# Whole weight rows for the first down product, stores on POOL's queue, sums on DVE

## The chip, the cores and the metric

The kernel runs on one core of a Trainium2 chip. The metric is device time in microseconds (us), of which the median of three runs is given. A profile of one further execution shows what each engine did when: TensorE (PE; its weight loads are shown as PEld), VectorE (DVE), ScalarE (ACT), GpSimd (POOL) and SyncE (SP), which in the kernel before issues all transfers. Each engine works through its own instructions in order.

## The reference

One step of a one-layer streaming encoder, for a prompt of 1024 positions and for 8 running streams of 16 positions each ("sample", 128 rows together). All arithmetic is in fp32.

```python
x = x + rmsnorm_pair(attention(h), s5_glu(h)) @ w_out      # h = rmsnorm(x) @ w_in
up = rmsnorm(x) @ w_up                                     # 1024 -> 2 x 2816
c = sum(up_padded[:, j:j+L] * conv_w[j] for j in range(3)) + conv_b
gate, val = split(c, 2)
x = x + (silu(gate) * val) @ w_down                        # 2816 -> 1024
y = rmsnorm(x) * final_g
```

Beside y it returns the new attention cache rows, the new state of the S5 recurrence and the new state of the convolution (the last two rows of `up` of each stream). The change touches the last three lines: how `w_down` is loaded and combined, how the gated values `g = silu(gate) * val` are stored and added, how the convolution's rows are stored, and how the last norms are scheduled.

## The kernel before

**Two stages matter here.** The up stage runs over 22 pairs `j` (one block of 128 gate columns and one of 128 value columns). Each pair is seven products (`product`, `collect`); `prep` splits the weights of the products ahead. In step 2 of the next pair `up_pair_end` does the convolution, the gate and the product g, and stores g to a scratch tensor: `g_d` for the prompt, `gs_d` for the sample. The down stage multiplies g (2816 long, 22 blocks, seen as two halves of `NK` = 11 blocks) with `w_down`.

**Splits.** A matmul of full precision is three matmuls on rounded operands (`mm3`): high times high, high times low, low times high. So each operand is first split in two: ACT writes the rounded high part (`wh`, `gh`), DVE subtracts it to get the low part (`wl`, `gl`). `operand` (lines 1522 to 1532) does this; the DVE half runs through the helper `tt` at line 86.

**The down product by seven.** The prompt's part is a 2 x 2 block product in seven products instead of eight (the Strassen-Winograd form). With the quarters g11 to g22 of g and B11 to B22 of `w_down`, the kernel runs them in this order: B11 with g11, T1 with S1, T2 with S2, B22 with S4, T3 with S3, B21 with g12, T4 with g22. Each is a loop over k of 11 steps with 12 matmuls of 512 columns a step. S1 is the sum of two quarters (`sum_one`, on POOL), and S2, S4 come from it by subtraction on DVE; S3 is the subtraction in the B22 loop at line 1710, `gr<-gr,gr` in the profile. T1 to T4 are sums of weight quarters: during the up stage `wd_load` fetches a block of them, `wd_sums` adds it up on DVE and stores it to the scratch tensor `t_d`, one block for each pair, 22 in all, in one buffer `ws`.

**The first product** (called the first down product below, lines 1643 to 1668) does two things at each step k: `p1_pairs` multiplies B11 with g11 for the prompt, and `p1_sample` multiplies all four quarters with the sample's g, which is too small to be worth the seven-product form. So it reads the whole of `w_down`, in blocks of 128 x 512 (256 KB): `w_op` loads a block into one of `WDB` = 5 buffers `wd` and splits it. The blocks B11 and B12 of a step are the two halves of the same 128 rows of 1024, as are B21 and B22.

**Order.** The program is written in one order, and a planner then orders the instructions of each engine by a simulated time: it may bring an instruction forward past ones written earlier, where its inputs are ready by its own estimate. `with tc.issue_after(x)` forbids it to put the block's instructions ahead of x on that engine. On the chip the order is fixed, and an instruction that waits holds up all behind it on its engine or queue. All transfers before are issued by SP, so a transfer that waits for a buffer holds up the following ones.

**Other pieces.** `conv_out` transposes the rows of the convolution state on TensorE, copies them with DVE into one of two buffers `cvr`, and stores them (seven times). The residual tiles `x3_0` to `x3_8` (128 x 1024) are loaded by `load_x` during T1 and T2, and a finished output is added to them by `drain`. `half_one` and `half_two` do the last norm: squares on ACT, the reciprocal root with a chain of small DVE operations (`rstd`), and the scaling. In the last product T4 the last five steps are held back and run tile by tile (`ops`), so that four row tiles finish one after the other.

```python
nc.sync.dma_start(g_d[j], g[:, 0:SEQ])
wd_sums(j - 1)                       # in pair j, step 1;  wd_load(j) in step 4
raw = dwA.tile([P, 512], F32, name=f"wd{w}", tag=f"wd{w % WDB}")
nc.gpsimd.tensor_tensor(SU[k], GA[1, 0, k], GA[1, 1, k], op=OP.add)
tt(GA[1, 0, k], GA[0, 0, k], GA[1, 0, k], OP.subtract)
half_two((NP2 + p,), HI, LO)
```

Of the kernel before, what the change touches and what calls it, by code (L numbers as in the profile page):

```python
# [18 lines left out]
P = 128  # L19
# [26 lines left out]
def emit(ctx, tc, x_prompt, x_sample, cache_k, cache_v, state_ssm_re, state_ssm_im, state_conv,  # L46
# [10 lines left out]
    def f(ap):  # L57
        return ap.bitcast(F32)
# [1342 lines left out]
    def up_pair_end(j):  # L1401
        cg = upw.tile([P, GLEN], F32, name=f"cg{j}", tag="cg", bufs=1)
        up_conv(j, 0, cg)
        act(cg, cg, AF.Silu)
        g = upw.tile([P, GLEN], F32, name=f"g{j}", tag="gs")
        up_conv(j, 1, g)
        tt(g, g, cg, OP.mult)
        nc.sync.dma_start(g_d[j], g[:, 0:SEQ])
        nc.sync.dma_start(gs_d[:, j], g[:, SEQ:])


    NK = NF // 2
# [40 lines left out]
    for i in range(7):  # L1453
        product(i, 1, pl0)
        collect(i, 1)
        prep(7 + i)
        if i == 3:
            wd_load(0)
    ps1.close()
    pups = ExitStack()  # L1460
    pup = pups.enter_context(pool("pup", 8, space=PSUM))
    for j in range(1, NF):
        load_up(j + 1)
        up_begin(j)
        for i in range(7):
            n = 7 * j + i
            for g in range(2):
                product(n, g)
                collect(n, g)
            prep(n + 7)  # L1470
            if i == 2:
                up_pair_end(j - 1)
            if i == 1:
                with tc.issue_after(LOW[min(n + 7, 7 * NF - 1)].ins):
                    wd_sums(j - 1)
            if i == 4:
                with tc.issue_after(UR[min(j + 1, NF - 1)].ins):
                    wd_load(j)
    wd_sums(NF - 1)
    up_pair_end(NF - 1)  # L1480
    fu.close()
    exs.close()
# [31 lines left out]
                    GS[q, k + i] = t[:, q, i]  # L1514

    def load_x(t):
        X3[t] = gr.tile([P, DM], F32, name=f"x3_{t}")
        nc.sync.dma_start(X3[t], x2_d[t * P:(t + 1) * P])

    CW, CG, SPARE, WD = [0], [0], [], {}  # L1520

    def operand(src, base, count, bufs, spare):
        w = count[0]
        count[0] += 1
        n = src.shape[-1]
        if spare:
            hi, lo = (gr.tile([P, n], F32R, name=f"{base}{x}{w}", tag=SPARE.pop()) for x in "hl")
        else:
            hi, lo = (dwA.tile([P, n], F32R, name=f"{base}{x}{w}", tag=f"{base}{x}{w % bufs}") for x in "hl")
        act(hi, src, AF.Copy)  # L1530
        tt(lo, src, f(hi), OP.subtract)
        return hi, lo

    def w_op(blk, k, spare=False):
        w = CW[0]
        raw = dwA.tile([P, 512], F32, name=f"wd{w}", tag=f"wd{w % WDB}")
        if blk[0] == "T":
            src = t_d[k, :, SUM_AT[blk]]
        else:
            r, e = (int(blk[1]) - 1) * NK + k, int(blk[2]) - 1  # L1540
            src = w_down[0, r * P:(r + 1) * P, e * 512:e * 512 + 512]
        WD[0] = nc.sync.dma_start(raw, src)
        return operand(raw, "w", CW, 4, spare)

    def g_op(src, spare=False):
        return operand(src, "g", CG, 2, spare)
# [4 lines left out]
    def conv_out():  # L1551
        cf = cvt.rearrange("p r a -> p (r a)")
        n = NROW * NF2
        outp = [(conv_prompt[0, 0].rearrange("j (a p) -> (j a) p", p=P), 0, 2 * NF2),
                (conv_sample[0].rearrange("b j (a p) -> (b j a) p", p=P), 2 * NF2, n - 2 * NF2)]
        for dst, c0, m_ in outp:
            for i in range(0, m_, P):
                m = min(P, m_ - i)
                pt = pdn.tile([P, P], F32, name=f"cvo{c0}_{i}", tag=f"b{(i // P) % 2}")
                nc.tensor.transpose(pt[:m], cf[:, c0 + i:c0 + i + m], ident)  # L1560
                r = dw.tile([P, P], F32, name=f"cvr{c0}_{i}", tag="rows", bufs=2)
                V_.tensor_copy(r[:m], pt[:m])
                nc.sync.dma_start(dst[i:i + m], r[:m])

    LO, HI = slice(0, 512), slice(512, DM)
    S3 = dw.tile([P, 2, NT], F32, name="S3")
# [43 lines left out]
    def sum_one(k):  # L1610
        if k < NK:
            SU[k] = gr.tile([P, 512], F32, name=f"su{k}", tag=f"su{k}")
            nc.gpsimd.tensor_tensor(SU[k], GA[1, 0, k], GA[1, 1, k], op=OP.add)


    smb, w11 = {}, {}

    def p1_pairs(k):
        w11[k] = w_op("B11", k)
        g = g_op(GA[0, 0, k])  # L1620
        for p in range(NP2):
            c = slice(p * P, (p + 1) * P)
            last = mm3(bank("a", p, k == 0), g[0][:, c], g[1][:, c], *w11[k], k == 0, k == NK - 1)
        return last

    def p1_sample(k):
# [8 lines left out]
        if k == 0:  # L1635
            for e in range(2):
                smb[e] = pdn.tile([P, 512], F32, name=f"dns{e}", tag=f"b{2 + e}")
        for blk in ("B11", "B12", "B21", "B22"):
            w = w11[k] if blk == "B11" else w_op(blk, k)
            q, e = int(blk[1]) - 1, int(blk[2]) - 1  # L1640
            mm3(smb[e], *sm[q], *w, k == 0 and q == 0, k == NK - 1 and q == 1)

    for k in range(NK):
# [62 lines left out]
    for k in range(NK):  # L1706
        w = w_op("B22", k)
        g = g_op(SU[k])
        pairs("b", k, g, w, False)
        tt(GA[1, 0, k], GA[0, 0, k], GA[1, 0, k], OP.subtract)  # L1710
        SPARE.append(f"su{k}")
    for p in range(NP2):
        drain("a", p, 0, HI)
# [33 lines left out]
    for p in range(NP2):  # L1747
        for k, (g, w) in ops.items():
            pairs("a", k, g, w, False, p)
        drain("a", p, 1, LO)  # L1750
        half_two((NP2 + p,), HI, LO)


_INS = ['x_prompt', 'x_sample', 'cache_k', 'cache_v', 'state_ssm_re', 'state_ssm_im', 'state_conv',
# [27 lines left out]
```

## Time and profile before

| what | us |
|---|---|
| median of 3 runs (lowest to highest) | 1218.39 (1217.08 to 1219.61) |
| the profiled execution's own time | 1217.93 |
| its span, first to last instruction | 1216.2 |
| TensorE busy in the span | 1161.7 |
| DVE busy | 943.3 |
| ACT busy | 658.2 |
| POOL busy | 256.6 |

All times in the text count from the start of the span. The up stage's last matmul is issued at about 949, the first down product runs to about 1020, T1 to about 1055, and the last matmul ends at 1205.7. A row of a view by stretches gives the stretch and its length, then for each engine busy time and number of instructions, then TensorE's granted clock as a share of full speed, the DMA engines' busy share, and GB/s. A row of waits reads: engine and tile, what it waited for, the total in us, how often, the longest. A row of a timeline gives start and duration in us, engine, line, operation, output and inputs, shapes. Names follow the kernel: `dna` and `dnb` are the down product's PSUM banks, `dns` the sample's, `su` the sums, `gr` the loaded quarters of g, `wd` the raw weights, `x` the residual tiles.

### The profile page before, as it was taken

The numbers are of one execution on the slowest core, as the hardware profiler recorded it, in microseconds if no ns is written. First come the engines' busy times: TensorE is split into PE (matmuls) and PEld (weight loads), VectorE is DVE, ScalarE is ACT, GpSimd is POOL, SyncE is SP. The second block draws the span as 40 slices with busy tenths as digits, with TensorE's granted clock in tenths as the row PEclk, the third lists the DMA queues.
The fourth block names the chain that finished last, engine by engine and source line by source line (L and its number), as shares of the span: only waits on it lengthen the run. The fifth ranks groups of instructions, "written<-read, shape, count | busy, mean of one in ns | idle before, by whom it ended". The sixth has DMA issues, their size and how long they took to land. (4 is left out here: it accounts for less than half of the span.)

```text
span 1216.2 us, 20649 instructions
## 1 busy us (share of the span) xinstructions
PE 1161.7 (96%) x7396; PEld 1022.7 (84%) x7396; DVE 943.3 (78%) x2061; ACT 658.2 (54%) x1417; POOL 256.6 (21%) x287
## 2 busy tenths in 40 slices
PE   8899999899989987999999999999999999999996
PEld 6777777677878767999999999999999776788885
DVE  6799768798437977887878878878787768977665
ACT  7246556763385776445455445454454555446553
POOL 0000000000000202644545545546442013000000
PEclk9899999899999989999999999999999999999998
DMA  8523226667723430334334243343333799842333
GB/s 256 111 81 129 91 69 179 201 210 210 216 70 139 140 136 29 115 116 139 104 126 141 90 142 126 110 140 108 127 125 118 247 309 332 302 139 92 96 102 139
DMA packets 165032, 177.89 MB, mean 146 GB/s; under 512 B 30618, under 2 KB 122402, under 8 KB 164898
## 3 DMA queue, kind: packets, MB, share of 16 engines
q1 hardware_dynamic: 164930, 176.58, 45.4%
q8 instruction: 58, 0.95, 0.3%
q14 instruction: 44, 0.36, 0.1%
HBM read 124.36 MB, written 53.23 MB: 146 GB/s over the span
## 5 line engine op out<-in xcount | busy, mean ns | idle before, releaser
L1307 DVE TENSOR_TENSOR op<-ur,op 128x512 fp32r<-128x512 f32 x132 | 121.7, 924 | 79.9 <-ACT op L1306 79.7
L1306 ACT ACTIVATE op<-ur 128x512 fp32r<-128x512 f32 x132 | 83.0, 632 | 92.0 <-POOL ur L1257 42.4
L1257 POOL TENSOR_TENSOR S<-ur 128x512 f32<-128x512 f32 x22 | 42.4, 1926 | 234.6 <-DMA ur<-in_w_up_dram 234.1
L1530 ACT ACTIVATE wh<-wd 128x512 fp32r<-128x512 f32 x110 | 68.4, 628 | 29.3 <-DMA wd<-in_w_down_dram 8.0
L86 DVE TENSOR_TENSOR wl<-wd,wh 128x512 fp32r<-128x512 f32 x110 | 74.2, 684 | 6.4 <-ACT wh L1530 6.3
L62 PE MATMUL dna<-wl,gh 128*128 128x512 f32 x176 | 70.1, 398 | 0.0
L61 PE MATMUL dna<-wh,gh 128*128 128x512 f32 x176 | 64.2, 396 | 3.9 <-ACT wh L1530 3.9
L1395 POOL COPY cvt<-ext 128x2 f32<-128x2 f32 x44 | 30.4, 690 | 158.4 <-DVE ext L86 158.4
L86 DVE TENSOR_TENSOR ws<-ws 128x256 f32<-128x256 f32 x88 | 56.1, 637 | 0.8 <-DVE ext L86 0.4
L63 PE MATMUL dna<-wh,gl 128*128 128x512 f32 x176 | 55.3, 397 | 0.0
L86 DVE TENSOR_TENSOR gl<-gr,gh 128x512 fp32r<-128x512 f32 x44 | 30.6, 695 | 30.8 <-PE dna L63 12.1
L62 PE MATMUL dnb<-wl,gh 128*128 128x512 f32 x132 | 50.4, 393 | 1.7 <-DVE wl L86 1.6
L61 PE MATMUL dnb<-wh,gh 128*128 128x512 f32 x132 | 49.0, 392 | 1.5 <-ACT wh L1530 0.9
L1530 ACT ACTIVATE gh<-gr 128x512 fp32r<-128x512 f32 x44 | 27.6, 630 | 36.4 <-PE dna L62 23.4
L1396 POOL COPY cvt<-ext 128x16 f32<-128x16 f32 x44 | 32.8, 746 | 63.4 <-ACT ext L1366 63.4
L1399 DVE SCALAR_TENSOR_TENSOR cg<-ext,cw,cg 128x1168 f32<-128x1168 f32 x22 | 44.5, 2022 | 0.0
L61 PEld LDWEIGHTS dna<-wh,gh 128*128 128x128 f32 x176 | 32.9, 189 | 11.8 <-ACT wh L1530 5.1
L1530 ACT ACTIVATE gh<-su 128x512 fp32r<-128x512 f32 x33 | 20.8, 632 | 36.7 <-PE dnb L62 19.0
L1257 POOL TENSOR_TENSOR ur<-S,ur 128x512 f32<-128x512 f32 x22 | 37.0, 1681 | 17.2 <-DVE op L1307 17.1
L62 PEld LDWEIGHTS dna<-wl,gh 128*128 128x128 f32 x176 | 34.0, 193 | 7.7 <-DVE wl L86 0.4
L63 PEld LDWEIGHTS dna<-wh,gl 128*128 128x128 f32 x176 | 33.9, 193 | 7.3
L1106 POOL MEMSET L<- 128x8 f32 x4 | 0.2, 112 | 181.1 <-PE pkv L62 181.1
(1278 smaller groups left out, 4366.9 us busy)
## 6 DMA issues: line engine op xcount, KB each, us to landing
ur<-in_w_up_dram SPq DMA_DIRECT2D x44, 512.0 KB, 4.7
wd<-in_w_down_dram SPq DMA_DIRECT2D x66, 256.0 KB, 3.8
ws<-in_w_down_dram SPq DMA_DIRECT2D x44, 256.0 KB, 3.4
g_d<-g SPq DMA_DIRECT2D x22, 512.0 KB, 2.6
t_d<-ws SPq DMA_DIRECT2D x22, 512.0 KB, 3.2
gr<-g_d SPq DMA_DIRECT2D x44, 256.0 KB, 6.1
wd<-t_d SPq DMA_DIRECT2D x44, 256.0 KB, 3.0
wa<-a_d SPq DMA_DIRECT2D x9, 512.0 KB, 3.5
```

Source lines behind the costliest of these rows:

```text
L61: mm(out, lh, rh, start=first, stop=False, skip_group_check=True)
L62: mm(out, lh, rl, start=False, stop=False, skip_group_check=True)
L63: return mm(out, ll, rh, start=False, stop=last, skip_group_check=True)
L86: V_.tensor_tensor(o, a, b, op=op)
L1106: nc.gpsimd.memset(L[q][:, :, 0], 0.0)
L1257: nc.gpsimd.tensor_tensor(o, a, b, op=op)
L1306: act(op[:, 0], src, AF.Copy)
L1307: LOW[n] = V_.tensor_tensor(op[:, 1], src, f(op[:, 0]), op=OP.subtract)
L1395: nc.gpsimd.tensor_copy(cvt[:, 0:2, ft], ext[:, SEQ:SEQ + 2])
L1396: nc.gpsimd.tensor_copy(cvt[:, 2:, ft].rearrange("p (b j) -> p b j", j=2), es[:, :, NS:])
L1399: stt(o, ext[:, 0:GLEN], cw[:, 0, ft:ft + 1], o, op0=OP.mult, op1=OP.add)
L1530: act(hi, src, AF.Copy)
```

## The change

It does six things.

1. `wd_load` and `wd_sums` run one pair earlier: the first block is loaded in step 0 of pair 0, added up in step 5, and the second loaded in step 6; nothing of them is left behind the last pair.
2. In the first down product, from step 2 on, each step loads two whole rows of weights (128 x 1024, 512 KB) with the new function `w_row` and splits their halves; in steps 0 and 1 only the lower row is loaded whole. The eight buffers are those of the residual tiles `x3_0` to `x3_7`, which are loaded later.
3. T1's first five loads are put behind the loads of rows 5 to 9 of the lower half on SP's queue.
4. The last pair's two stores of g and the seven stores of convolution rows are issued by POOL instead of SP.
5. `sum_one` runs on DVE instead of POOL, and the subtraction for S3 is put behind the low split of its own step (`LO_[0]`).
6. The reciprocal roots of the first two of the last four row tiles are taken together.

```diff
-        nc.sync.dma_start(g_d[j], g[:, 0:SEQ])
-        nc.sync.dma_start(gs_d[:, j], g[:, SEQ:])
+        q = nc.gpsimd if j == NF - 1 else nc.sync
+        q.dma_start(g_d[j], g[:, 0:SEQ])
+        q.dma_start(gs_d[:, j], g[:, SEQ:])
...
-        if i == 3:
+        if i == 0:
             wd_load(0)
+        if i == 5:
+            wd_sums(0)
+        if i == 6:
+            wd_load(1)
...
-                    wd_sums(j - 1)
-            if i == 4:
+                    wd_sums(j)
+            if i == 4 and j < NF - 1:
                 with tc.issue_after(UR[min(j + 1, NF - 1)].ins):
-                    wd_load(j)
-    wd_sums(NF - 1)
+                    wd_load(j + 1)
...
-        tt(lo, src, f(hi), OP.subtract)
+        LO_[0] = V_.tensor_tensor(lo, src, f(hi), op=OP.subtract)
...
+        if blk == "T1" and k < WDB:
+            with tc.issue_after(ROW[1, NK - 1 - WDB + k].ins):
+                WD[0] = nc.sync.dma_start(raw, t_d[k, :, SUM_AT[blk]])
+            return operand(raw, "w", CW, 4, spare)
...
+    def w_row(q, k):
+
+        CR[0] += 1
+        raw = gr.tile([P, DM], F32, name=f"wr{q}{k}", tag=f"x3_{CR[0] % NPT}")
+        r = (q * NK + k) * P
+        ROW[q, k] = WD[0] = nc.sync.dma_start(raw, w_down[0, r:r + P])
+        return raw
...
-                nc.sync.dma_start(dst[i:i + m], r[:m])
+                nc.gpsimd.dma_start(dst[i:i + m], r[:m])
...
-            nc.gpsimd.tensor_tensor(SU[k], GA[1, 0, k], GA[1, 1, k], op=OP.add)
+            tt(SU[k], GA[1, 0, k], GA[1, 1, k], OP.add)
...
-        w11[k] = w_op("B11", k)
+        if k < 2:
+            w11[k] = w_op("B11", k)
+        else:
+            rows[0, k], rows[1, k] = w_row(0, k), w_row(1, k)
+            w11[k] = operand(rows[0, k][:, 0:512], "w", CW, 4, False)
...
+        if k < 2:
+            rows[1, k] = w_row(1, k)
+        for q, e in ((0, 0), (0, 1), (1, 0), (1, 1)):
+            if q == e == 0:
+                w = w11[k]
+            elif (q, k) in rows:
+                w = operand(rows[q, k][:, e * 512:e * 512 + 512], "w", CW, 4, False)
+            else:
+                w = w_op(f"B{q + 1}{e + 1}", k)
...
-        tt(GA[1, 0, k], GA[0, 0, k], GA[1, 0, k], OP.subtract)
+        with tc.issue_after(LO_[0].ins):
+            tt(GA[1, 0, k], GA[0, 0, k], GA[1, 0, k], OP.subtract)
...
-        half_two((NP2 + p,), HI, LO)
+        if p:
+            half_two((NP2, NP2 + 1) if p == 1 else (NP2 + p,), HI, LO)
```

More of the change, by code (lines that the diff above doesn't have):

```diff
@@ L1516, in load_x @@
     def load_x(t):
-        X3[t] = gr.tile([P, DM], F32, name=f"x3_{t}")
+        X3[t] = gr.tile([P, DM], F32, name=f"x3_{t}", tag=f"x3_{t}")
         nc.sync.dma_start(X3[t], x2_d[t * P:(t + 1) * P])
-    CW, CG, SPARE, WD = [0], [0], [], {}
+    CR, CW, CG, SPARE, WD, LO_, ROW = [0], [0], [0], [], {}, {}, {}
     def operand(src, base, count, bufs, spare):
@@ L1612, in sum_one @@
             SU[k] = gr.tile([P, 512], F32, name=f"su{k}", tag=f"su{k}")
-            nc.gpsimd.tensor_tensor(SU[k], GA[1, 0, k], GA[1, 1, k], op=OP.add)
-    smb, w11 = {}, {}
+            tt(SU[k], GA[1, 0, k], GA[1, 1, k], OP.add)
+    smb, w11, rows = {}, {}, {}
     def p1_pairs(k):
-        w11[k] = w_op("B11", k)
+        if k < 2:
[3 more added lines that the diff above has]
+            w11[k] = operand(rows[0, k][:, 0:512], "w", CW, 4, False)
         g = g_op(GA[0, 0, k])
@@ L1637, in p1_sample @@
                 smb[e] = pdn.tile([P, 512], F32, name=f"dns{e}", tag=f"b{2 + e}")
-        for blk in ("B11", "B12", "B21", "B22"):
-            w = w11[k] if blk == "B11" else w_op(blk, k)
-            q, e = int(blk[1]) - 1, int(blk[2]) - 1
+        if k < 2:
[7 more added lines that the diff above has]
+                w = w_op(f"B{q + 1}{e + 1}", k)
             mm3(smb[e], *sm[q], *w, k == 0 and q == 0, k == NK - 1 and q == 1)
```

## The prediction

> **What bounds the kernel now.** I first read busy time by stretches, cut at TensorE's stalls around the down product, with TensorE (PE), weight loads, DVE, ACT and POOL, then granted clock, DMA share and GB/s:
>
> ```profile
> 949.50:1020.20 70.70, 65.98 (x272) 51.63 (x272) 52.93 (x98) 41.32 (x81) 9.24 (x8) 0.95 0.89 296
> 1020.20:1055.00 34.80, 31.65 (x132) 23.95 (x131) 33.31 (x58) 15.62 (x28) 7.81 (x6) 1.00 0.88 308
> 1085.00:1205.70 120.70, 120.69 (x532) 99.50 (x530) 78.06 (x148) 65.01 (x119) 0.00 (x0) 1.00 0.30 99
> 1205.70:1216.20 10.50, 0.00 (x0) 0.00 (x0) 6.11 (x25) 2.78 (x5) 0.00 (x0) 0.61 0.49 197
> ```
>
> The third stretch runs 532 matmuls of 512 columns in 120.7 us, 0.227 us each, with nothing between them: TensorE is the bound there, and the change leaves that stretch alone. At this rate the first product (11 steps of 24 matmuls, 264 in all, and about 0.4 us of small transposes) would need 60.3 us. It takes 70.7, so 10.4 us are lost. The T1 product (132 matmuls, 30.0 us) takes 34.8 and loses 4.8. With the 10.5 us from the last matmul to the end, these 25.7 us are the reach of the change; before 949.5 it only moves small work.
>
> What TensorE's weight loads waited for, first in 949 to 1020.3 and then in 1020.2 to 1060 (us, times, longest):
>
> ```profile
> PEld dna L61 <- ACT wh L1530: 5.1, 4, 2.2
> PEld dns L61 <- ACT wh L1530: 1.6, 3, 0.9
> PEld dns L62 <- DVE wl L86: 0.8, 2, 0.5
> PEld dna L62 <- DVE wl L86: 0.4, 1, 0.4
> ...
> PEld dnb L62 <- DVE wl L86: 3.4, 4, 1.1
> PEld dnb L61 <- ACT wh L1530: 1.4, 2, 1.3
> PEld dnb L61 <- DVE x L86: 1.1, 1, 1.1
> ```
>
> In the first product it waits for ACT's rounded weights, in T1 for DVE's remainders. ACT itself waited for weights to land (first row); the next two are the landing of one 256 KB load (median, then minimum, median, maximum):
>
> ```profile
> ACT wh L1530 <- DMA wd<-in_w_down_dram: 8.0, 10, 2.4
> ...
> wd<-in_w_down_dram SPq DMA_DIRECT2D x66, 256.0 KB, 3.8
> ...
> DMA to landing us min/median/max: 2.5/3.5/7.5
> ```
>
> The stalls cost twice, since the clock drops after a long one. Matmuls that should start 0.227 us apart start 0.43 us apart at two places (two rows from the timeline, two from the chain of waits):
>
> ```profile
> 954.16 0.63 PE L62 MATMUL dna<-wl,gh 128*128 128x512 f32 x1
> 954.59 0.63 PE L63 MATMUL dna<-wh,gl 128*128 128x512 f32 x1
> ...
> 987.25 0.43 PE dna L62
> 987.67 0.43 PE dna L63
> ```
>
> Five such matmuls follow the stall at 949 and eight the one at 983: 1.0 and 1.6 us.
>
> **The change part by part.** *The last weight sums come one pair earlier.* Now the last sums stand on SP's queue ahead of the first weight load; SP's and ACT's timelines:
>
> ```profile
> 940.87 1.45 SPq L1425 DMA_DIRECT2D ws<-in_w_down_dram  x2
> 946.79 0.56 SPq L1435 DMA_DIRECT2D t_d<-ws  x1
> 947.40 1.62 SPq L1542 DMA_DIRECT2D wd<-in_w_down_dram  x2
> ...
> 949.66 1.36 ACT L1397 ACTIVATE g<-ext,cw 128x1168 f32<-128x1168 f32 x1
> 951.01 0.63 ACT L1530 ACTIVATE wh<-wd 128x512 fp32r<-128x512 f32 x1
> ```
>
> Both issues at 940.87 and the store at 946.79 go, so the first weight load can stand where 940.87 is, some 6 us sooner, and has landed before TensorE asks at 949.5. Late next is then only ACT and DVE splitting the first operands (0.63 and 0.69 us). Of 2.1 us of stall I take 1.5, and the 1.0 us of slow clock, which a short stall does not show: **-2.5 us** (ends 0, if the load's memory is free no sooner, and -3.1).
>
> At the other end, pair 0 gains one set of four subtractions and a store, and the next load behind that store on SP. In steady state each pair keeps one set, one load and one store. DVE in 445 to 482, and the subtraction (min/median/max ns):
>
> ```profile
> 445.00:482.00 37.00, 26.91 (x170) 24.98 (x169) 29.18 (x65) 26.16 (x63) 7.42 (x7) 0.91 0.19 57
> ...
> L86 DVE TENSOR_TENSOR ws<-ws x88: 407/414/1514, 494.0 to 946.3; 128x256 f32<-128x256 f32 x88
> ```
>
> TensorE is idle 10.1 us of these 37, waiting for ACT and DVE, so four times 0.41 us can land on the path: **+0.7 us** (ends 0, in DVE's idle 7.8 us, and +1.7).
>
> *Whole weight rows.* From step 2 on, two loads of 512 KB replace four of 256 KB a step (20 rows in all, 18 of them in pairs), with eight buffers in place of five half-size ones: 4 MB ahead instead of 1.3. ACT and DVE split the same blocks. Five loads of T1's weights (1.3 MB) also move ahead, behind rows 5 to 9. The bytes stay, and the engines are already 0.89 busy, so either rate or timing must improve. Two 10 us stretches, one with 2 KB rows alone, one in which 4 KB rows of x3 mix in:
>
> ```profile
> 1006.00:1016.00 10.00, 10.00 (x46) 8.26 (x45) 7.62 (x14) 5.79 (x12) 2.71 (x2) 1.00 0.91 294
> 1052.00:1062.00 10.00, 10.00 (x46) 8.29 (x45) 8.49 (x14) 5.05 (x8) 0.00 (x0) 1.00 1.04 397
> ...
> 950.00:956.00 6.00, 4.31 (x12) 3.16 (x13) 5.92 (x8) 5.37 (x10) 0.86 (x2) 0.72 0.96 325
> 956.00:966.00 10.00, 9.44 (x40) 7.04 (x39) 9.22 (x17) 4.82 (x9) 0.00 (x0) 1.00 0.66 219
> ```
>
> Per full share that is 323 against 382 GB/s. From 949.5 to 1020.2, 296 GB/s moved 20.9 MB. With T1's 1.3 MB that is 22.2 MB, 10.5 of them in rows: 27.5 us at 382 and 36.2 us at 323, 63.7 together, 5.0 us less than all at 323, and it need no longer pause, as at 956 to 966 (0.66), when a buffer is waited for. It is still more than the product's 60.3, so I do not count on all of its stalls to go.
>
> A rule of the Trainium skill speaks against this part (DMA: Bandwidth & Descriptors, Specifications): transfers of 512 B and more already run at line rate. By it a 4 KB row is no faster than a 2 KB one, and this edit would give only its buffers. The two stretches above differ by 18%, though their order of loads differs too, so the trace does not settle it.
>
> The landing stalls are worth 5.1 - 2.1 = 3.0 us of the first row, about 0.9 of the second and third, and the 1.6 us of slow clock: 5.5 us. The other 1.4 us are ACT and DVE with the last pair's convolution (DVE 5.92 of 6 us busy from 950) and stay. I take **-4.0** (ends 0 and -5.5).
>
> *Gated sums and the pinned subtractions.* DVE in 1020.2 to 1055 by shape, then POOL's sums, their waits, and DVE's wait for them:
>
> ```profile
> L86 DVE TENSOR_TENSOR gl<-su,gh 128x512 fp32r<-128x512 f32 x11 | 8.8, 800 | 0.8 <-PE dnb L63 0.8
> L86 DVE TENSOR_TENSOR su<-su,gr 128x512 f32<-128x512 f32 x10 | 7.9, 788 | 0.0
> L86 DVE TENSOR_TENSOR gr<-gr,gr 128x512 f32<-128x512 f32 x6 | 5.1, 848 | 2.3 <-POOL su L1613 2.3
> ...
> L1613 POOL TENSOR_TENSOR su<-gr,gr x11: 1277/1312/2415, 988.6 to 1031.7; 128x512 f32<-128x512 f32 x11
> ...
> POOL su L1613 <- DMA gr<-g_d: 59.5, 10, 37.4
> DVE gr L86 <- POOL su L1613: 3.7, 2, 2.3
> ```
>
> DVE is busy 33.3 of 34.8 us. Six subtractions for a much later product (`gr<-gr,gr`) sit in T1 and cost 5.1 us and 2.3 of waiting for POOL; the change pins all eleven behind the B22 product's own splits, where DVE has room (in 1085 to 1205.7 it is busy 65%). The other shapes are stretched beyond 0.68 us (800 and 788 ns) while POOL reads too: 1.3 and 1.1 us. In exchange eleven sums come to DVE at 0.68 us, eight of them written in T1: 5.4 us. The balance is 9.8 - 5.4 = 4.4 us off DVE in T1, and T1's first weights have landed. TensorE loses 4.8 here; I take **-3.5** (ends +2 and -4.8: a sum that waits for its data now holds up the splits behind it).
>
> *POOL's queue.* Nine stores leave SP for POOL: the last pair's two and seven rows of the convolution state. On SP a row's issue and landing are
>
> ```profile
> L1563 SPq DMA_DIRECT2D out_dram<-cvr x7: 333/366/593, 984.5 to 1003.5; - x7
> ...
> DMA to landing us min/median/max: 3.0/3.9/4.9
> ```
>
> SP has 3 us less to issue and no longer waits for DVE's copies. No DMA in this trace is issued by POOL. If one costs what SP's does, POOL, idle after the last pair, hides it; the end then waits for one more queue. I take 0 (ends -0.5 and +1.5).
>
> *Roots 2+1+1.* The last four tiles' square roots run as one pair and two singles: two roots of nine small DVE operations each become one of twelve (the wider form takes two operations where a column as scalar takes one). DVE at the end:
>
> ```profile
> 1205.73 0.69 DVE L86 TENSOR_TENSOR x<-x,dna 128x512 f32<-128x512 f32 x1
> 1208.69 0.15 DVE L130 SCALAR_TENSOR_TENSOR rsa<-S 128x1 f32<-128x1 f32 x1
> 1211.61 0.75 DVE L1589 SCALAR_TENSOR_TENSOR x<-x,rs,fgb 128x512 f32<-128x512 f32 x1
> ```
>
> The last root starts 3.0 us after its drain though ACT's square needs about 1.5; at best 2.2 us go. But the pair's root starts only when its second tile is drained. I take **-0.5** (ends +1 and -2.2).
>
> **Sum.** -2.5 + 0.7 - 4.0 - 3.5 + 0 - 0.5 = -9.8 us. The profiled execution took 1217.93 us (span 1216.2, 1.7 around it), so 1208.1; the median of the runs is 0.46 above it: 1208.6.
>
> **The rivals.**
>
> *The first product stays bound by bytes.* The share of 0.89 speaks for it, the stretch at 397 GB/s against it. The 4.0 goes: 1212.6. (The Trainium skill's line-rate rule above, DMA: Bandwidth & Descriptors, Specifications, would bring this case about.)
>
> *T1 stays bound by DVE:* the sums fill what the subtractions left, drains and the sample tile's root come forward into it. The 33.3 of 34.8 us speak for it, the 4.4 us balance against it. The 3.5 goes: 1212.1.
>
> *It doesn't do what it says:* the instruction order is planned again, the first load or the rows wait for memory of the up stage and SP stands still behind them. Starts and rows give nothing, T1's gain is lost to new orders: 1218.
>
> *DVE takes over POOL's waits (the slower side).* POOL waited 59.5 us for the summands; without the first 37.4, 22.1 in nine waits. POOL had nothing else to do, DVE has the splits behind it. If all of it lands on the path, 22.1 - 9.8 = 12.3 us slower: 1230.7. It decides from 1.1 us a sum. Against it: summands are loaded three to five steps ahead, and rows no longer hold SP up.
>
> *POOL's queue is late:* DVE's copy of a row needs the store of two before it. Seven copies in 981.7 to 1002.9 leave about 7 us for a landing of 3.9 and its issue; twice the landing (8.2 us with the issue) would hold DVE 1.1 us at each of five copies: 5.5 us, 1214.1. The Trainium skill (SBUF — State Buffer, SBUF: two separate sides) says that POOL writes its descriptors through a port that DVE can lock; no run here shows it yet.
>
> **How the numbers follow.** Forecast 0.48, bytes 0.18, DVE in T1 0.12, nothing 0.08, DVE waits 0.08, POOL's queue 0.06. The measurement tells 0.2%, 2.4 us, from no change. Faster: 0.48 + 0.18 + 0.12 + 0.05 = 0.83; same 0.08; slower 0.09. All ends on the good side give about 1202.9. The range of 1203 to 1216 takes in the bytes, T1 and POOL cases and leaves out the other two.
>
> **What would show it.** Right: the first weight load issued near 941; TensorE's gap at the end of the up stage under 1 us, without 0.43 us matmuls; the first product near 64 us; T1 near 31; no `gr<-gr,gr` before B22; the pause after the last drain shorter. Wrong: DMA share near 0.9 with ACT waiting for rows, DVE waiting for `gr<-g_d`, copies of `cvr` waiting for POOL's stores, or new stalls in pair 0.

## The result and the profile after

In five alternating runs of each kernel the changed one took 1210.78 us (median, 1208.66 to 1213.23), the one before 1217.21 (1215.55 to 1219.61). The ratio is 0.9945, 95% interval 0.9927 to 0.9963: 6.4 us less, where 9.8 were forecast. The time lies in the range of 1203 to 1216, 2.2 us above the forecast.

The profiled execution of the changed kernel took 1213.23 us (span 1211.4), the longest of its five. These are its stretches, in the columns of the prediction's first fence; the second to fifth rows are cut at the same events as the four rows there, the first row and the last serve later parts:

```profile
949.00:967.00 18.00, 14.38 (x53) 10.08 (x52) 17.00 (x27) 12.01 (x22) 2.12 (x4) 0.91 0.83 290
949.10:1017.20 68.10, 64.08 (x271) 50.45 (x271) 57.21 (x104) 41.90 (x83) 4.47 (x9) 0.97 0.95 357
1017.20:1050.90 33.70, 31.80 (x133) 25.72 (x133) 26.79 (x53) 14.96 (x27) 1.45 (x3) 0.95 0.72 233
1080.90:1201.60 120.70, 120.68 (x532) 99.45 (x530) 82.70 (x156) 64.28 (x118) 0.00 (x0) 1.00 0.32 99
1201.60:1211.40 9.80, 0.00 (x0) 0.00 (x0) 5.86 (x21) 3.39 (x6) 0.00 (x0) 0.64 0.54 214
979.00:1009.00 30.00, 29.60 (x132) 23.95 (x131) 24.78 (x50) 17.06 (x36) 1.79 (x4) 1.00 1.04 395
```

The up stage ends 0.4 us sooner (949.10 for 949.50), the first product with the pause before it lost 2.6 (68.1 for 70.7), T1 with the pause before it 1.1 (33.7 for 34.8), the end 0.7 (9.8 for 10.5); 532 matmuls take 120.7 us as before. Together 4.8, and the two profiled executions stand 4.7 apart. The first 0.4 are not the change's: the up stage lasts 506.2 us before and 506.1 after, from its first weight load (443.2 and 442.9) to its last. DVE is busy 26.8 us in T1 where it was busy 33.3: T1 is no longer its stage. In the first 18 us of the first product, though, DVE is busy 17.0.

What TensorE's weight loads waited for, in 949 to 1017.9 (five rows) and in 1017.8 to 1056 (two rows):

```profile
PEld dna L61 <- ACT wh L1534: 3.3, 4, 1.9
PEld dns L61 <- ACT wh L1534: 2.0, 2, 1.7
PEld dns L62 <- DVE wl L1535: 0.8, 1, 0.8
PEld dna L62 <- DVE wl L1535: 0.6, 1, 0.6
PEld cvo L1576 <- DVE cvr L1578: 0.4, 1, 0.4
...
PEld dnb L61 <- issue: 2.3, 1, 2.3
PEld dnb L61 <- ACT gh L1534: 0.2, 1, 0.2
```

Of T1's waits for DVE's remainders nothing is left; one pause of 2.3 us stands at its start, and behind it eight matmuls at 0.43 us (1.6 us). The tile view of `dnb` names DVE's additions into `x`, which free the sample's banks, for 1.9 us of that pause. Six of the kernels below (`rows_on_sp`, `own_buffer_count`, `last_conv_on_pool`, `cg_taps_first` and the two of the last section) pass from the first product to T1 in 1.7 to 2.5 us and show no slow matmuls there. So part of the distance between this execution's 4.7 us and the 6.4 of the medians may be the slow clock.

The pause at the start of the first product stayed. SP's timeline, then ACT's:

```profile
940.46 1.28 SPq L1550 DMA_DIRECT2D wd<-in_w_down_dram  x2
...
948.22 1.15 ACT L1534 ACTIVATE gh<-gr 128x512 fp32r<-128x512 f32 x2
949.26 1.36 ACT L1397 ACTIVATE g<-ext,cw 128x1168 f32<-128x1168 f32 x1
950.51 0.62 ACT L1534 ACTIVATE wh<-wd 128x512 fp32r<-128x512 f32 x1
...
955.78 0.63 ACT L1534 ACTIVATE gh<-gr 128x512 fp32r<-128x512 f32 x1 [1.56 <-issue]
958.77 1.18 ACT L1404 ACTIVATE cg<-cg 128x1168 f32<-128x1168 f32 x1 [2.35 <-DVE cg L1399]
```

The first weight load does go out at 940.46 (947.40 before), as forecast. But `wh` is rounded at 950.51, straight behind the first tap of the last pair's value (`g`, 1.36 us), and TensorE pauses as long as before. At 958.77 ACT stands 2.35 us at the last pair's Silu; the roundings of the first whole rows are queued behind it.

The end, in DVE's timeline, from the last drain to the last scaling:

```profile
1201.62 0.69 DVE L86 TENSOR_TENSOR x<-x,dna 128x512 f32<-128x512 f32 x1
...
1207.04 0.75 DVE L1605 SCALAR_TENSOR_TENSOR x<-x,rs,fgb 128x512 f32<-128x512 f32 x1
```

That is 5.4 us where it was 5.9 (1205.73 to 1211.61).

### The profile page after: what moved, and what is told of

The parts are those of the page before. It is cut to its first block, busy times and chain, and to the rows that moved or that the text cites. A ratio compares the mean times of both kernels' runs of the same rounds, so it can differ in the third digit from the quotient of the medians.

```text
span 1211.4 us, 20557 instructions
## 1 busy us (share of the span) xinstructions
PE 1160.0 (96%) x7396; PEld 1023.2 (84%) x7396; DVE 944.8 (78%) x2065; ACT 657.4 (54%) x1417; POOL 244.8 (20%) x285
## 5 line engine op out<-in xcount | busy, mean ns | idle before, releaser
L1395 POOL COPY cvt<-ext 128x2 f32<-128x2 f32 x44 | 30.3, 689 | 158.4 <-DVE ext L86 158.4
L61 PE MATMUL dnb<-wh,gh 128*128 128x512 f32 x132 | 52.3, 396 | 1.9 <-DVE x L86 1.9
L1535 DVE TENSOR_TENSOR gl<-gr,gh 128x512 fp32r<-128x512 f32 x44 | 30.4, 690 | 29.1 <-PE dna L63 12.0
L1534 ACT ACTIVATE wh<-wd 128x512 fp32r<-128x512 f32 x70 | 43.9, 630 | 15.1 <-PE dnb L63 8.0
L1535 DVE TENSOR_TENSOR wl<-wd,wh 128x512 fp32r<-128x512 f32 x70 | 47.7, 686 | 0.1
L1396 POOL COPY cvt<-ext 128x16 f32<-128x16 f32 x44 | 32.8, 746 | 64.1 <-ACT ext L1366 64.1
L61 PEld LDWEIGHTS dna<-wh,gh 128*128 128x128 f32 x176 | 32.8, 189 | 10.1 <-ACT wh L1534 3.3
L1257 POOL TENSOR_TENSOR ur<-ur,ur 128x512 f32<-128x512 f32 x22 | 36.9, 1679 | 1.7
```

What stands on the lines that cost most here:

```text
L61: mm(out, lh, rh, start=first, stop=False, skip_group_check=True)
L1257: nc.gpsimd.tensor_tensor(o, a, b, op=op)
L1395: nc.gpsimd.tensor_copy(cvt[:, 0:2, ft], ext[:, SEQ:SEQ + 2])
L1396: nc.gpsimd.tensor_copy(cvt[:, 2:, ft].rearrange("p (b j) -> p b j", j=2), es[:, :, NS:])
L1535: LO_[0] = V_.tensor_tensor(lo, src, f(hi), op=OP.subtract)
```

## The experiments

Every kernel here was timed in rounds beside the kernel before. The ratios' intervals are 0.3 to 0.4% wide, so between two variants a difference under some 3 us is not told by the times; the traces tell the stages apart. The right part of the table is worked out from the trace of one execution each, in us, between starts of TensorE's weight loads: from the last of the up stage to the first of `dna` (start), from there to the last of `dns` (first product), to the first of `dnb` (change-over), to the first `dna` of T2 (T1), and from the last load to the end of the span (end). "Stalls" between two times, counted from the end of the up stage, are what these starts lie further apart than 0.23 us; a matmul at the slow clock counts 0.2 in them. Of the kernel before and the changed one they are 1.4 and 3.2 us between 9 and 18 us, and 5.2 and 0.8 between 18 and 60.

| kernel | median | ratio to before (95%) | start | first product | change-over | T1 | end |
|---|---|---|---|---|---|---|---|
| before | 1217.21 | | 2.3 | 68.5 | 1.5 | 33.8 | 11.1 |
| changed | 1210.78 | 0.9945 (0.9927-0.9963) | 2.1 | 66.1 | 2.6 | 31.6 | 10.5 |
| rows_on_sp | 1211.52 | 0.9960 (0.9946-0.9974) | 2.1 | 66.1 | 2.1 | 30.0 | 10.5 |
| four_row_buffers | 1209.57 | 0.9943 (0.9923-0.9962) | 2.1 | 66.8 | 0.2 | 30.7 | 10.5 |
| own_buffer_count | 1209.43 | 0.9943 (0.9927-0.9960) | 2.1 | 66.0 | 2.1 | 30.0 | 10.5 |
| last_conv_on_pool | 1212.30 | 0.9966 (0.9952-0.9980) | 0.9 | 69.9 | 2.1 | 30.5 | 10.5 |
| half_rows | 1212.23 | 0.9967 (0.9951-0.9983) | 2.1 | 65.1 | 1.0 | 33.8 | 10.7 |
| no_whole_rows | 1209.67 | 0.9937 (0.9919-0.9955) | 2.1 | 64.8 | 0.7 | 30.5 | 10.7 |
| cg_taps_first | 1210.77 | 0.9948 (0.9929-0.9968) | 2.1 | 66.3 | 1.7 | 30.3 | 10.5 |
| sums_on_pool | 1210.91 | 0.9956 (0.9937-0.9974) | 2.1 | 66.1 | 2.5 | 30.3 | 10.5 |
| pool_stores_alone | 1217.13 | 1.0007 (0.9995-1.0020) | 2.2 | 66.9 | 0.2 | 34.9 | 11.2 |
| whole_rows_alone | 1228.07 | 1.0097 (1.0078-1.0115) | 2.7 | 77.7 | 1.9 | 32.8 | 10.8 |
| no_rows_four_buffers | 1211.47 | 0.9952 (0.9935-0.9968) | 2.1 | 65.6 | 0.6 | 31.4 | 10.7 |
| sums_dve_unpinned | 1211.10 | 0.9947 (0.9928-0.9965) | 2.1 | 66.9 | 1.9 | 30.4 | 10.5 |

The traces differ most where the kernels do not. The first weight load of the up stage comes anywhere from 438.7 to 444.6 us, but from it to that stage's last load 505.8 to 506.3 us pass in all fourteen, and from the first `dna` of T2 to the last load 149.6 us in all but `whole_rows_alone` (150.6). So the five columns, and their sum, compare two traces better than the total times do; each still stands for one execution.

### The pause at T1's start

`rows_on_sp`:

```diff
-                nc.gpsimd.dma_start(dst[i:i + m], r[:m])
+                nc.sync.dma_start(dst[i:i + m], r[:m])
```

> The changed kernel with the seven rows of the convolution state stored from SP's queue again; nothing else is edited. In the trace of the changed kernel DVE's copies of these rows stand at 982.1, 986.1, 1005.4, 1008.3, 1016.4, 1020.2 and 1022.2 us (before the change 981.7 to 1002.9), and T1's first matmul finds its banks taken: 2.2 us of TensorE at rest and eight matmuls at 0.43 us, 3.7 us in all. Theory (two buffers and the order pace the copies, whichever queue stores them): the copies stay late, the stall at T1 stays, time within 1.5 us of the changed kernel's 1210.8. Rival (POOL's queue itself is what is late): copies end before 1010 us, the stall at T1 is under 1 us, time about 1207.

`four_row_buffers`:

```diff
-                r = dw.tile([P, P], F32, name=f"cvr{c0}_{i}", tag="rows", bufs=2)
+                r = dw.tile([P, P], F32, name=f"cvr{c0}_{i}", tag="rows", bufs=4)
```

> The changed kernel with four buffers in place of two for the copied rows of the convolution state, still stored from POOL's queue. Theory (a copy waits for the store of two rows before, so the last transposes and copies hold two of T1's banks, and the sample product holds the two others it could start on): the copies end before 1010 us, T1 starts on the banks that the transposes used, the pause of 2.2 us at 1017.7 us goes and the eight matmuls of 0.43 us behind it; 3 to 3.7 us faster than the changed kernel's 1210.8, about 1207.4. Rival (T1 waits for DVE's splits or for the late tile of x anyway): the pause only gets another name, time within 1 us of 1210.8.

DVE's copies of the convolution rows, by line (minimum, median and maximum in ns, first and last start): the changed kernel, with the rows on SP, with four buffers, and, from the section on whole rows, without them.

```profile
L1578 DVE COPY cvr<-cvo x7: 276/284/285, 982.1 to 1022.2; 128x128 f32<-128x128 f32 x5, 88x128 f32<-88x128 f32 x1, 64x128 f32<-64x128 f32 x1
```

```profile
L1578 DVE COPY cvr<-cvo x7: 276/282/284, 982.5 to 1021.6; 128x128 f32<-128x128 f32 x5, 88x128 f32<-88x128 f32 x1, 64x128 f32<-64x128 f32 x1
```

```profile
L1578 DVE COPY cvr<-cvo x7: 276/283/284, 977.8 to 1005.9; 128x128 f32<-128x128 f32 x5, 88x128 f32<-88x128 f32 x1, 64x128 f32<-64x128 f32 x1
```

```profile
L1574 DVE COPY cvr<-cvo x7: 273/284/284, 982.4 to 1002.0; 128x128 f32<-128x128 f32 x5, 88x128 f32<-88x128 f32 x1, 64x128 f32<-64x128 f32 x1
```

The last copies come as late from SP's queue as from POOL's, so the queue is not the cause, and the rival fell. With four buffers the planner puts all seven before 1006 (61 us behind the end of the up stage, where the last one comes 73 us behind it in the changed kernel), T1 starts on the two banks that the transposes have left, and the change-over falls from 2.1-2.6 to 0.2 us. The stalls move in part: first product and T1 are each some 0.7 us longer than in `rows_on_sp`. In time the 3.4 us expected did not show (1209.57). In the last row there are only two buffers, but no whole rows, and the copies end at 1002: the late copies come with the whole rows. The other kernels agree: with whole rows and two buffers the last copy starts at 1018.8 us or later in each, without the rows at 1002.9 or sooner. That the planner reckons with long landings beside those rows, and so spaces the two-buffered copies, is the likely link; no trace shows its estimates.

### The start of the first product

`own_buffer_count` (the half-row loads get their buffer from a counter `CB` of their own):

```diff
-        w = CW[0]
+        w = CB[0]
+        CB[0] += 1
         raw = dwA.tile([P, 512], F32, name=f"wd{w}", tag=f"wd{w % WDB}")
```

> The changed kernel with the buffers of the half-row loads counted by themselves, so that the load of B12's block of step 1 no longer falls on the first buffer again, which in the changed kernel it gets only at 952.7 us, with the whole rows behind it on SP's queue (the first at 954.3 us). Theory (the rows start late because SP stands at that load): the first whole row is issued near 949.3 us, the stalls of 4.1 us between 959.4 and 965 shrink by 2 to 4 us; time about 1208. Rival (these stalls are ACT's and DVE's work with the last pair's convolution, or the bytes in flight): the rows are issued sooner and TensorE's stalls stay; time within 1 us of 1210.8.

SP's timeline; the up stage ends 2.1 us sooner in this execution (946.9 for 949.0):

```profile
946.51 1.07 SPq L1551 DMA_DIRECT2D wd<-in_w_down_dram  x2
947.63 0.53 SPq L1515 DMA_DIRECT2D gs<-gs_d  x1
948.20 0.60 SPq L1508 DMA_DIRECT2D gr<-g_d  x1
948.84 0.91 SPq L1559 DMA_DIRECT2D wr<-in_w_down_dram  x2
```

The first row goes out 1.9 us behind the end of the up stage, in the changed kernel it was 5.3 (954.30). Nothing follows: TensorE's stalls between 9 and 18 us behind that end are 3.2 us in both, and the first product takes 66.0 us for 66.1. The rival held: late rows were not the cause.

`last_conv_on_pool`:

```diff
-        act(o, ext[:, 2:], AF.Identity, bias=cw[:, 3, ft:ft + 1], scale=cw[:, 2, ft:ft + 1])
+        if j == NF - 1 and i == 1:
+            nc.gpsimd.tensor_scalar(o, ext[:, 2:], cw[:, 2, ft:ft + 1], cw[:, 3, ft:ft + 1], op0=OP.mult, op1=OP.add)
+        else:
+            act(o, ext[:, 2:], AF.Identity, bias=cw[:, 3, ft:ft + 1], scale=cw[:, 2, ft:ft + 1])
```

> The changed kernel with one operation moved: the first tap of the last pair's second convolution, 1.36 us on ACT right ahead of the first rounded weight block, is done by POOL. Theory (the start of the first product is held by the order of ACT's work, not by the landing of the weights, which went out at 940.5 us): TensorE's pause of 2.1 us at 949 us falls to 0.8 us or less and the five matmuls of 0.43 us behind it go; about 2.3 us faster than 1210.8, 1208.5. Rival (my prediction's reason, the landing): the pause stays, since the load had long landed it is then DVE's remainders and the gated sum of the last pair that hold it; time within 0.8 us of 1210.8.

ACT's, DVE's and POOL's timelines:

```profile
946.32 1.15 ACT L1537 ACTIVATE gh<-gr 128x512 fp32r<-128x512 f32 x2
947.36 0.63 ACT L1537 ACTIVATE wh<-wd 128x512 fp32r<-128x512 f32 x1
...
946.98 1.71 DVE L1538 TENSOR_TENSOR gl<-gr,gh 128x512 fp32r<-128x512 f32 x1 [0.35 <-ACT gh L1537]
...
946.84 1.31 POOL L1398 TENSOR_SCALAR g<-ext,cw 128x1168 f32<-128x1168 f32 x1
```

ACT's order is what held TensorE: with the tap gone `wh` follows `gh`, and the pause falls from 2.1 to 0.9 us. But the first product takes 69.9 us for 66.1. DVE's remainder beside POOL's tap took 1.71 us instead of 0.69, and between 9 and 18 us TensorE now stalls 5.4 us for 3.2. The likely reading is that a sooner start only brings TensorE sooner to the place where ACT and DVE are behind with the last pair; the run does not separate this from what POOL's tap itself costs DVE. So half of the theory held (the order), its gain did not.

`cg_taps_first` (`TAP[0]` is the gate's last tap):

```diff
...
+        if j == NF - 1 and i == 1:
+            with tc.issue_after(TAP[0].ins):
+                V_.scalar_tensor_tensor(o, ext[:, 0:GLEN], cw[:, 0, ft:ft + 1], o, op0=OP.mult, op1=OP.add)
...
```

> The changed kernel with one order pinned on DVE: the last tap of the last pair's gate comes before the last tap of the last pair's value, so that ACT's Silu of the gate, on which ACT stands 2.4 us with four weight blocks queued behind it, can start some 2 us sooner (956.7 for 958.8 us). Theory (TensorE's stall of 3.2 us between 9 and 18 us behind the end of the up stage comes from ACT's queue standing at this Silu): the stall falls to 1 to 1.8 us, about 1.7 us faster than 1210.8. Rival (DVE has too much to do there, whatever its order: four taps, a product and the remainders): the stall moves to the remainders and stays at 3 us; time within 0.8 us of 1210.8.

ACT's waits in 947 to 965:

```profile
ACT sh L1656 <- PE dns L62: 1.8, 1, 1.8
ACT gh L1538 <- issue: 1.5, 1, 1.5
ACT wh L1538 <- PE dns L63: 0.6, 1, 0.6
ACT cg L1408 <- DVE cg L1403: 0.5, 1, 0.5
```

The wait at the Silu falls from 2.4 to 0.5 us, and TensorE's stalls between 9 and 18 us from 3.2 to 2.5: 0.7 us, where 1.7 were expected. ACT's next wait is for TensorE itself, 1.8 us, for the buffer of a sample split. 0.7 us of stalls appear at 45 to 60 us; the time is unchanged. The Silu is one link, not the whole cause. That DVE is busy 17.0 of the first 18 us does not explain the rest: it is busy 16.4 of them in the kernel before and 16.8 in `no_whole_rows`, with stalls of 1.4 and 2.2 us. Why the stalls are 3.2 us with the rows stays open.

### Whole rows

`half_rows`:

```diff
-        ROW[q, k] = WD[0] = nc.sync.dma_start(raw, w_down[0, r:r + P])
+        for c in (slice(0, 512), slice(512, DM)):
+            ROW[q, k] = WD[0] = nc.sync.dma_start(raw[:, c], w_down[0, r:r + P, c])
```

> The changed kernel with each whole weight row fetched by two transfers of half a row (2 KB lines) into the same buffer; buffers, bytes and order of use stay. Theory (my prediction's reason: 4 KB lines move faster, 382 against 323 GB/s per full DMA share): between 20 and 60 us behind the end of the up stage the GB/s per full DMA share fall by some 15%, TensorE waits for rows again, 2 to 4 us slower than the changed kernel's 1210.8. Rival (the Trainium skill, DMA: Bandwidth & Descriptors, Specifications: lines of 512 B and more run at line rate; it was the depth of the buffers): the rate stays within 5%, the stalls in that stretch stay at the changed kernel's 0.8 us, time within 1 us of 1210.8.

Thirty us of the first product with rows in two halves; the answering row of the changed kernel is the last of the first fence above:

```profile
977.40:1007.40 30.00, 30.00 (x136) 24.65 (x135) 23.56 (x49) 17.12 (x36) 2.16 (x4) 1.00 1.04 379
```

Per full share of the DMA engines that is 379/1.04 = 364 GB/s in lines of 2 KB against 395/1.04 = 380 in lines of 4 KB: 4%, not the 18% I took from two stretches of before, and TensorE does not wait for a row at all there. The rival held. By the same measure `no_whole_rows`, below, makes 341/0.99 = 344 GB/s from five half-size buffers: the deeper buffers, with T1's early loads, are worth 6%, the longer lines 4%. The Trainium skill's rule (DMA: Bandwidth & Descriptors, Specifications), by which lines of 512 B and more are all at line rate, comes within these 4% of the measurement. T1 (33.8 us) waits 3.5 us for two copies of convolution rows, of which the planner put the last as late as 1023.3.

`no_whole_rows`:

```diff
-        if blk == "T1" and k < WDB:
...
-        if k < 2:
-            w11[k] = w_op("B11", k)
-        else:
-            rows[0, k], rows[1, k] = w_row(0, k), w_row(1, k)
-            w11[k] = operand(rows[0, k][:, 0:512], "w", CW, 4, False)
+        w11[k] = w_op("B11", k)
...
-        if k < 2:
-            rows[1, k] = w_row(1, k)
```

> The changed kernel without whole rows: all four weight blocks of a step are loaded as half rows through the five buffers of before, and T1's weights are not fetched ahead; the other parts of the change stay. Theory (rows took away the landing stalls in the middle and brought none themselves at the start): TensorE's stalls between 18 and 60 us behind the end of the up stage come back to 4 to 5 us (0.8 with rows), those between 9 and 18 us fall from 3.2 to about 1.4: 2 to 3 us slower than 1210.8. Rival (SP's queue, freed of the convolution rows, was enough): the stalls in the middle stay near 1 us, and the time is 1 to 2 us better than 1210.8.

Its waits of TensorE's weight loads in 949 to 1047, and the same thirty us:

```profile
PEld dna L61 <- ACT wh L1534: 2.7, 3, 1.9
PEld dns L62 <- DVE wl L1535: 2.0, 5, 0.5
PEld dns L61 <- ACT wh L1534: 2.0, 4, 0.9
PEld dnb L61 <- ACT wh L1534: 1.0, 2, 0.5
...
979.00:1009.00 30.00, 30.00 (x137) 24.51 (x136) 23.44 (x48) 17.98 (x36) 3.79 (x7) 1.00 0.99 341
```

Without the rows TensorE is busy all of these 30 us, on 341 GB/s where the rows moved 395: the extra bandwidth served nothing. The rows do bring weights sooner: from the end of the up stage to T1, ACT waits 5.9 us for weights to land without them and 2.1 us for rows with them. Little of that reaches TensorE: its stalls that were to return between 18 and 60 us are 2.0 us, and those between 9 and 18 us fall from 3.2 to 2.2. The first product is 1.3 us shorter than with rows, of which 1.0 is five matmuls at 0.43 us that this execution did not have; the change-over is 0.7 us for 2.1-2.6. Time 1209.67: no different. In the middle the rival was nearer (near 1 us, where the theory had 4 to 5).

`whole_rows_alone` (the kernel before with the parts of the change's diff that concern `w_row`, the tags of x3 and T1's early loads):

```diff
...
+            rows[0, k], rows[1, k] = w_row(0, k), w_row(1, k)
+            w11[k] = operand(rows[0, k][:, 0:512], "w", CW, 4, False)
...
```

> The kernel before with one part of the change alone: from step 2 on the first product's weights are loaded as whole rows into the x3 buffers, T1's first five weight blocks behind rows. Theory (the same as for the stores alone: either part takes away the stalls in the middle, and together they gain them once): the stalls between 18 and 60 us fall to about 1 us, the ones between 9 and 18 us rise to 3 us, first product 66 us, 2 to 3 us faster than before. Rival (rows give nothing as long as the convolution rows stand on SP's queue): middle stalls stay at 4 us or more, within 1 us of before.

SP's waits and timeline, then DVE by shape in 1003 to 1010, where POOL adds gated sums:

```profile
SPq L1408 <- DVE sl L86: 8.0, 1, 8.0
...
950.44 0.52 SPq L1511 DMA_DIRECT2D gs<-gs_d  x1
958.75 0.33 SPq L1408 DMA_DIRECT2D g_d<-g  x1
959.12 0.43 SPq L1409 DMA_DIRECT2D gs_d<-g  x1
959.59 0.72 SPq L1504 DMA_DIRECT2D gr<-g_d  x1
960.36 0.94 SPq L1553 DMA_DIRECT2D wr<-in_w_down_dram  x2
...
L86 DVE TENSOR_TENSOR gr<-gr,gr 128x512 f32<-128x512 f32 x2 | 3.5, 1774 | 0.0
```

Neither theory foresaw this: 11.3 us slower than the runs of before beside it (1216.79). SP stands 8.0 us at the store of the last pair's g, and the first row goes out only behind it, at 960.36; one stall of 8.0 us follows on TensorE, then slow matmuls, and at 1005.7 another of 3.2 us, where two subtractions take 1.77 us each beside POOL's additions. So the last pair's store on POOL's queue, which I costed at nothing, is what the rows stand on. The 8.0 us are traced to that store; no run puts it alone back on SP in the changed kernel, so how much of the 11.3 it makes is not shown.

### POOL's queue alone, and the best candidate

`pool_stores_alone` (the kernel before with the two edits of `dma_start` to POOL):

```diff
+        q = nc.gpsimd if j == NF - 1 else nc.sync
...
-                nc.sync.dma_start(dst[i:i + m], r[:m])
+                nc.gpsimd.dma_start(dst[i:i + m], r[:m])
```

> The kernel before with one part of the change alone: the seven rows of the convolution state and the last pair's two stores go out from POOL's queue. Theory (SP's queue, where the weight loads stood behind stores that waited for DVE's copies, made the landing stalls in the middle of the first product): TensorE's stalls between 18 and 60 us behind the end of the up stage fall from 5.2 to about 2 us and the 1.6 us of slow clock there go; first product some 65.5 us for 68.5, T1 as before at 33 to 34; 2.5 to 4 us faster than before. Rival (my prediction: worth nothing): within 1 us of before.

The median does not move (ratio 1.0007). In the trace the first product is 1.7 us shorter, mainly since the eight matmuls at 0.43 us (1.6 us) are missing; the stalls between 18 and 60 us fall from 5.2 to 2.8 us, others rise; the change-over is 1.2 us shorter (1.47 to 0.23) and T1 1.1 us longer. By the time, the prediction's 0 is right and my new theory's 2.5 to 4 wrong.

`no_rows_four_buffers` joins the edits of `no_whole_rows` and `four_row_buffers`.

> The changed kernel without whole rows (as in the run without them, which took 1209.7 us) and with four buffers for the convolution rows: the version that the runs so far point to. Theory (both effects stand beside each other): first product 64.8 us or less, T1's first pauses of 0.6 to 0.7 us shrink since two of its banks are free sooner; 1208.5 to 1209.5, faster than both kernels. Rival (the order planned anew costs what the buffers bring): 1209.7 to 1211, no better than the changed kernel.

It took 1211.47 us, 1.8 above `no_whole_rows`, which the times do not tell apart. In the trace the two gains do not add up: the columns' sum is 110.4 us where it is 108.8 without the four buffers (1.0 of the difference is five slow matmuls), and a pause of 1.6 us stands just behind T1's first load. No version tried is measurably faster than the changed kernel by its time.

### Sums and subtractions

`sums_on_pool` and `sums_dve_unpinned`, in this order:

```diff
-            tt(SU[k], GA[1, 0, k], GA[1, 1, k], OP.add)
+            nc.gpsimd.tensor_tensor(SU[k], GA[1, 0, k], GA[1, 1, k], op=OP.add)
...
-        with tc.issue_after(LO_[0].ins):
-            tt(GA[1, 0, k], GA[0, 0, k], GA[1, 0, k], OP.subtract)
+        tt(GA[1, 0, k], GA[0, 0, k], GA[1, 0, k], OP.subtract)
```

> The changed kernel with the eleven gated sums back on POOL, the eleven subtractions still pinned behind the B22 product's splits. Theory (the pinned subtractions alone freed T1; DVE has room without the sums): T1 takes 30.0 to 30.6 us, as in the runs of the changed kernel whose clock didn't drop there, and the time is within 1 us of 1210.8. Rival (my prediction's balance: POOL's reads stretch DVE's operations and its sums come late): T1 takes 31 us or more, DVE's shapes there are near 0.8 us for 0.68, and TensorE waits for roundings of sums: 1 to 2.5 us slower.

> The changed kernel with the eleven subtractions for the S3 product no longer pinned behind the B22 product's splits; the gated sums stay on DVE. They then stand in T1 and T2 in DVE's order. Theory (the pin freed T1, the sums' place matters little, as the run with the sums on POOL showed): the subtractions that come into T1 cost TensorE there about what they did before the change, T1 32 to 34 us and the time 2 to 3.5 us above the changed kernel's 1210.8. Rival (taking the sums off POOL is enough: without POOL's reads beside them DVE's operations take 0.68 us, the subtractions no longer wait for POOL's sums and fit): T1 at 30 to 31 us, time within 1 us of 1210.8.

POOL's sums in the first, DVE's subtractions in the second, by tile:

```profile
L1629 POOL TENSOR_TENSOR su<-gr,gr x11: 1286/1485/1820, 976.8 to 1011.0; 128x512 f32<-128x512 f32 x11
```

```profile
L86 DVE TENSOR_TENSOR gr<-gr,gr x11: 681/684/693, 981.0 to 1017.5; 128x512 f32<-128x512 f32 x11
```

T1 is 30.3 and 30.4 us: in the changed kernel each half of this part is enough alone. No run undoes both. With the sums on POOL they are done by 1012.5, ahead of T1. With the subtractions unpinned and no sums on POOL, the planner puts them into the first product, at 0.68 us each, and that grows by 0.8 us. So the theory held for the first kernel, the rival for the second.

That this part (5 in the list of the change) carries most of the gain is told by three kernels in a chain. `pool_stores_alone` is the kernel before with part 4. `no_whole_rows` has parts 1, 4, 5 and 6. The changed kernel adds the rows, parts 2 and 3. Along it the five columns add up to 117.2 us before, then 115.4, 108.8 and 112.9. So by the traces the stores take 1.8 us, of which 1.6 is slow clock; parts 1, 5 and 6 take 6.6; and the rows give 4.1 back, of which 2.6 are thirteen slow matmuls that the execution of `no_whole_rows` did not have. The ratios to before are 1.0007, 0.9937 and 0.9945: they confirm the middle step, and do not tell the other two from nothing. Of the 6.6 us, the start has 0.1, where part 1 was to act, and the end 0.5, which is part 6. Change-over and T1 together fall by 3.9, the first product by 2.1 (1.0 of it slow clock); that these come from part 5 is what is left, since parts 1 and 6 act elsewhere. No run takes parts 1 or 6 back alone.

## Why the prediction landed in its range, and which of its steps failed

**The sum** was 3.4 us too large, and its largest term, the rows', was not there. That the time lies in the range is in part luck: the rows were to give 4.0 us and gave none, and part 5, down for 3.5 us in T1, gave more by the chain above, some of it in the first product.

- *Last weight sums earlier, -2.5.* The start moved 0.1 us. The step that failed is "Late next is then only ACT and DVE splitting the first operands". The load did land early, but ACT had the last pair's tap ahead of `wh`. My own fence showed it: `g` at 949.66 for 1.36 us, `wh` at 951.01 with no idle before it. `last_conv_on_pool` confirms the order as cause; there the gain did not last, though POOL's tap has a part in that. At the other end pair 0 cost nothing where 0.7 was taken: the up stage, from its first weight load to its last, takes 506.1 us for 506.2.
- *Whole rows, -4.0.* The first product lost 2.5 us, but not by rows: without them it is as short or shorter. Two steps failed. The rates of 323 and 382 GB/s were put down to the length of the lines, and of these 18% `half_rows` leaves 4%. And TensorE's stalls were taken to end with more buffers. ACT's waits for landing do fall with the rows (5.9 to 2.1 us), but most of TensorE's stalls in the middle end without them. The stores alone shorten the first product by 1.7 us in their trace, nearly all of it slow clock, and parts 1 and 5 by another 2.1; how that divides between sums and pin was not separated. Rows bring the late copies of the convolution rows with them, and with these the change-over. (One figure of this term does not come out: by the rows of the fence, 1.9 us were left to "stay", not 1.4; no forecast hangs on it.)
- *Gated sums and pinned subtractions, -3.5.* T1 fell from 33.8 to 31.6, and to 30.0-30.7 in most of the variants, which lack the slow matmuls: 3.1 to 3.8, the size forecast. The stretch that the term was read from begins with the pause ahead of T1, though, and that pause grew by 1.1 us with the rows; in the changed kernel's trace the stretch fell by 1.1 only (33.7 for 34.8). The balance of 5.4 us of sums against 9.8 counted both edits as needed; either was enough.
- *POOL's queue, 0.* Right by the time for this edit alone. What I did not see is that it is the precondition of the rows: left on SP in `whole_rows_alone`, the last pair's store holds the queue 8.0 us, and that kernel is 11 us slower than before.
- *Roots, -0.5.* Right: from the last drain to the last scaling 5.4 us pass in each of the eleven kernels with this part and 5.9 in each of the three without it.

**The rivals.** *The first product stays bound by bytes* had 1212.6, as near to the measured 1210.8 as the forecast's 1208.6 within the noise, and its 4.0 did go, but not for its reason: the share of 0.95 looks like a bound by bytes, and yet 341 GB/s feed the same product. *T1 stays bound by DVE* fell: DVE is busy 26.8 of T1's 33.7 us. *It doesn't do what it says* was right on the start and the rows, which give nothing, though for other reasons, and wrong on T1. *DVE takes over POOL's waits* fell: DVE's waits in the changed kernel from 949 to 1060 have one row for it.

```profile
DVE su L86 <- DMA gr<-g_d: 0.2, 1, 0.2
```

*POOL's queue late* named the right buffers, the two for the copied rows, but the wrong culprit: the copies' order is set by the planner, it is as late with SP's stores, and DVE's waits there have no row for a store. The end named for all terms on the good side, 1202.9, should be 1202.3: the good ends add up to -16.1 us.

## What to carry to other kernels

When a wait names an operand of ACT, look at what ACT did just before it: if it had no idle time, its order holds the operand, and an earlier transfer gives nothing. A rise in GB/s is no gain where TensorE was not waiting for bytes; take the transfer size back alone before crediting it. And test the parts of a change alone: one may be a precondition (the last store off SP's queue), two may gain the same microseconds once (the sums and the pin). Last, compare traces from the point where the kernels begin to differ: here up to 6 us between two executions lie ahead of it.

## What the runs showed of the hardware

- POOL's work can hold DVE up. In `whole_rows_alone` two subtractions took 1.77 us each while POOL added, against 0.68 alone. In `last_conv_on_pool` a remainder took 1.71 us for 0.69, and POOL's tap ran beside its first 1.17. The Trainium skill (SBUF — State Buffer, SBUF: two separate sides) describes a lock that DVE and POOL hold for a whole instruction, the other one waiting; the 1.02 us that the remainder lost beside 1.17 of the tap agree with it.
- The clock's drop does not follow from the pause alone. TensorE's timelines at the start, of the changed kernel and of `no_whole_rows`:

```profile
951.19 1.69 PE L61 MATMUL dna<-wh,gh 128*128 128x512 f32 x4 [1.75 <-ACT wh L1534]
...
953.76 0.63 PE L62 MATMUL dna<-wl,gh 128*128 128x512 f32 x1
954.19 0.63 PE L63 MATMUL dna<-wh,gl 128*128 128x512 f32 x1
```

```profile
951.11 1.20 PE L61 MATMUL dna<-wh,gh 128*128 128x512 f32 x4 [1.75 <-ACT wh L1534]
...
953.47 0.39 PE L63 MATMUL dna<-wh,gl 128*128 128x512 f32 x1
953.69 0.40 PE L62 MATMUL dna<-wl,gh 128*128 128x512 f32 x1
```

  Both paused 1.75 us; the first then ran matmuls 0.43 us apart, at a granted clock of 0.50 (953.3 to 955), the second 0.23 apart, at 1.00. A microsecond or more of a stage can hang on this, so a difference of that size between two single traces proves little.
- POOL issued a store of a convolution row in 0.54 us, and it landed after 4.8 us (median of seven), where in the kernel before SP needed 0.37 and 3.9.
